# 256-token stages of a two-block transformer: high and low activations as one 512-column operand

## The chip, the cores and the metric

The kernel runs on one core of a Trainium2 chip. The metric is the device time of one execution in microseconds (us); less is better. The engines of a core work beside each other, each on an instruction queue of its own that it takes in order: TensorE (PE in the profile; PEld is its weight loads), VectorE (DVE), ScalarE (ACT), GpSimd (POOL), and SyncE (SP), whose queue issues the DMA loads of the weights.

## The reference

Everything is float32, with one batch of 256 latent tokens and width 1024. A first block of two layers works on the latent tokens and on 256 context tokens together; the context is dropped inside the second layer, after its mixer. A second block of one layer works on the 256 latent tokens alone. Cut to what the change touches:

```
swiglu(h, w_in, w_out):  a, b = split(h @ w_in);  return (silu(a) * b) @ w_out        # 1024 -> 2 x 2816 -> 1024

first_block, layer i = 0, 1:
    x_lat, x_ctx += 0.5 * gate * swiglu(modulate(x), ffn_a)
    o_l, o_c = mixer(h_l, h_c)        # neighbourhood attention + long convolution (0), retention (1)
    x_lat += gate * o_l
    x_lat += 0.5 * gate * swiglu(modulate(x_lat), ffn_b_in[i], ffn_b_out[i])
    # x_ctx likewise, but not after the mixer of layer 1

second_block:
    x = x + 0.5 * swiglu_2(rms_norm_2(x, g_ffn1), w_ffn1_gu, w_ffn1_down)
    q, k, v = split(rms_norm_2(x, g_mix) @ w_in)          # 16 heads: 12 dilated, 4 block attention
    x = x + concat(rms_norm_2(oa), rms_norm_2(ob)) @ w_out
    x = x + memory_cross_attention(x, mem, ...)           # q = h @ w_cq, k, v = mem_norm @ w_ckv, out @ w_co
    x = x + 0.5 * swiglu_2(rms_norm_2(x, g_ffn2), w_ffn2_gu, w_ffn2_down)
    return rms_norm_2(x, g_final)
```

## The kernel before

**Layout.** Activations lie with features on the partitions, in blocks of 128, and tokens along the row: `x[0]` to `x[7]` are the residual stream. The first block's joint stages have 512 token columns (latent and context); the stages behind the mixer of layer 1 have 256. These 256-token stages are: the second feed-forward of layer 1, both feed-forwards of block 2, the q and k projections of its mix, the memory keys (`mem_piece`), and the query and output projections of the cross attention.

**High and low parts.** Each float32 operand is kept as two parts in a reduced type: `split` has ScalarE copy the value into the high part (L152) and VectorE subtract that from the value into the low part (L153). A product of one block of K (128 features) with one block of 128 outputs is `mm3`, three matmuls into one PSUM accumulation: low weight by high activation (L200), high by low (L201), high by high (L202). For a 512-token stage the parts are tiles of their own; for 256 tokens, `pair` puts the high part into the left and the low part into the right half of one 512-column tile (tiles `h` for inputs, `g` for the products of the feed-forward).

**Weights.** SP loads them into `st` tiles (6 buffers); `split` makes `w` tiles of them (22 buffers), each [128, 512], so that one holds the high or the low parts for four products. A split can be made when TensorE has freed a `w` tile. PSUM has four tags, `pa` to `pd`, with two buffers of one bank, [128, 512], each.

**Feed-forward** (`ffn`). The 22 column blocks go in three groups (`GROUPS`: 8, 8 and 6 blocks), and within a group by pairs. For each block, eight products go into `pa` (gate) and eight into `pb` (up). The result is evacuated by VectorE and ScalarE into the tiles `t1` and `t2` (L645 without, L647 to L650 with a norm), and split into `g`. After each group `project_out` multiplies its `g` blocks with the rows of the second weight that belong to them, output block by output block into `pc`, and `residual` adds each bank to its `x` tile (L562). In the last group the sums of squares of the new `x` are gathered in `acc` (L350, L353, L354).

**Late norm.** In block 2 the reciprocal root mean square is not known yet when a stage starts. `norm_late` scales `x` by the gain and splits it (L517, L518); the sums over `acc` on TensorE (L205, into `pd`), the power on GpSimd (L365) and the spread over the partitions (copied at L537 into `rb[1]`) come while the first products already run: `settle` puts them behind certain accumulations, and the first four accumulations take K blocks 0 to 5 first, 6 and 7 later. The factor `rb[1]`, one for each token, is multiplied at the evacuation. The feed-forward of layer 1 has its norm applied beforehand (`rb` is None).

**Three lines elsewhere** that the rows show: L1352 is ScalarE's copy of a bank of memory keys; in the mix's attention, L1261 is GpSimd's addition of bias tables in SBUF and L1281 VectorE's scaling of the probabilities.

**Order.** The program is written in the order above; Tile's scheduler then puts the instructions of each engine in order, by their dependences and place in the program. So an engine's queue mixes stages, for instance weight splits for later products between the evacuations of this one.

## Time and profile before

| | before |
|---|---|
| time, median of 3 runs (lowest to highest) | 2554.69 us (2551.87 to 2554.76) |
| span of the profiled execution, from the first to the last instruction | 2549.0 us |
| the span's distance to the median | 5.7 us |
| TensorE busy | 2515.0 us (99%) |
| VectorE busy | 1751.8 us (69%) |
| ScalarE busy | 1109.4 us (44%) |
| GpSimd busy | 70.8 us (3%) |
| read from HBM | 382.8 MB, 153 GB/s over the span |
| chain of work that ended last | 82% of it TensorE |

Of the profiled execution the time between its first and its last instruction is known, and it is 2549.0 us; what lies around it is seen only as the distance to the runs' median. An engine counts as busy from the start of an instruction to its end; matmuls overlap, and their ends are modelled, so the distance from start to start says more on TensorE's pace than its busy time. A name such as L200 is a line of the kernel before; the rows of one line can have more than one shape.

### The profile page before, as it was taken

What the parts mean: (1) busy time and instruction counts of PE and PEld (TensorE: products, weight loads), DVE (VectorE), ACT (ScalarE), POOL (GpSimd) and SP (SyncE); (2) the same over time, 40 slices, a digit from 0 to 9 for tenths busy, and PEclk for the clock granted to TensorE, in tenths of its full rate; (3) what the DMA queues carried; (4) which work ended last, traced back from release to release, by engine and by line L of the source; (5) the groups of instructions that cost most, each with busy time, mean ns of one, the idle gap of its engine ahead of it and who ended that gap; (6) DMA issues with size and microseconds to landing.
All of it is one profiled execution on the core that took longest, in us unless ns stands there. A gap on an engine that the chain in (4) does not pass through costs nothing.

```text
span 2549.0 us, 39425 instructions
## 1 busy us (share of the span) xinstructions
PE 2515.0 (99%) x14967; PEld 2176.7 (85%) x14967; DVE 1751.8 (69%) x3443; ACT 1109.4 (44%) x2164; POOL 70.8 (3%) x95
## 2 busy tenths in 40 slices
PE   8998999999999999999999999999999999999999
PEld 5786778857987888988788888889999999789998
DVE  6896875577887747777533846667667667676775
ACT  4322224364432323432322635546556555665554
POOL 0000000210000000000000000000000000300000
PEclk9998999999999999999999999999999999999999
DMA  7575653331355635365422524435556556544553
GB/s 270 193 225 158 194 187 96 95 83 50 100 174 181 190 116 157 115 197 179 143 83 90 167 83 133 133 113 190 181 174 194 182 172 195 164 132 142 183 184 98
DMA packets 345133, 388.44 MB, mean 152 GB/s; under 512 B 22123, under 2 KB 294720, under 8 KB 344944
## 3 DMA queue, kind: packets, MB, share of 16 engines
q1 hardware_dynamic: 341752, 380.75, 47.6%
q10 hardware_dynamic: 3192, 5.18, 0.8%
q8 instruction: 117, 1.92, 0.3%
q14 instruction: 72, 0.59, 0.1%
HBM read 382.80 MB, written 6.23 MB: 153 GB/s over the span
## 4 chain that ended last, share of the span: by engine, by line
PE 82%; issue 8%; DVE 5%; DMA 4%; ACT 1%; POOL 0%; SPq 0%; POOLq 0%; DVEq 0%; ACTq 0%
PE pa L200 11%; PE pa L201 11%; PE pa L202 11%; PE pc L200 8%; PE pc L201 8%; PE pc L202 8%; PE pb L200 6%; PE pb L201 6%; PE pb L202 6%; DMA st<-in_w_mod_dram 2%; PE pb L205 2%; DVE t L308 2%; PE pc L205 2%; PE pd L205 1%; DVE w L153 1%
## 5 line engine op out<-in xcount | busy, mean ns | idle before, releaser
L152 ACT ACTIVATE w<-st 128x512 fp32r<-128x512 f32 (+1 forms) x1136 | 693.3, 620 | 872.3 <-PE pc L200 272.4
L153 DVE TENSOR_TENSOR w<-st,w 128x512 fp32r<-128x512 f32 (+1 forms) x1136 | 761.0, 677 | 340.0 <-ACT w L152 327.6
L200 PE MATMUL pa<-h,w 128*128 128x256 f32 (+1 forms) x1544 | 514.1, 333 | 0.2 <-ACT h L401 0.2
L202 PE MATMUL pa<-h,w 128*128 128x256 f32 (+1 forms) x1544 | 509.8, 330 | 0.0
L200 PE MATMUL pc<-g,w 128*128 128x256 f32 (+1 forms) x1404 | 444.0, 317 | 4.1 <-DVE w L153 1.7
L201 PE MATMUL pc<-g,w 128*128 128x256 f32 (+1 forms) x1404 | 443.1, 316 | 0.9 <-DVE g L153 0.9
L202 PE MATMUL pc<-g,w 128*128 128x256 f32 (+1 forms) x1404 | 441.8, 315 | 0.0
L201 PE MATMUL pa<-h,w 128*128 128x256 f32 (+1 forms) x1352 | 439.4, 325 | 0.0
L200 PE MATMUL pb<-h,w 128*128 128x256 f32 (+1 forms) x1120 | 371.0, 331 | 0.0
L202 PE MATMUL pb<-h,w 128*128 128x256 f32 (+1 forms) x1120 | 370.5, 331 | 0.0
L308 DVE SCALAR_TENSOR_TENSOR t<-st,cs,t 128x512 f32<-128x512 f32 x448 | 319.3, 745 | 40.9 <-DMA st<-in_w_mod_dram 39.3
L200 PEld LDWEIGHTS pa<-h,w 128*128 128x128 f32 x1544 | 294.0, 191 | 42.8 <-ACT w L152 8.7
L202 PEld LDWEIGHTS pa<-h,w 128*128 128x128 f32 x1544 | 294.1, 191 | 30.1 <-issue 4.6
L201 PE MATMUL pb<-h,w 128*128 128x256 f32 (+1 forms) x928 | 298.6, 322 | 0.0
L200 PEld LDWEIGHTS pc<-g,w 128*128 128x128 f32 x1404 | 267.2, 191 | 25.7 <-issue 5.4
L201 PEld LDWEIGHTS pc<-g,w 128*128 128x128 f32 x1404 | 267.8, 191 | 18.7 <-DVE g L153 2.4
L202 PEld LDWEIGHTS pc<-g,w 128*128 128x128 f32 x1404 | 267.7, 191 | 16.6
L201 PEld LDWEIGHTS pa<-h,w 128*128 128x128 f32 x1352 | 258.0, 191 | 24.7 <-issue 5.9
L200 PEld LDWEIGHTS pb<-h,w 128*128 128x128 f32 x1120 | 213.0, 190 | 20.1 <-DVE w L153 0.7
L202 PEld LDWEIGHTS pb<-h,w 128*128 128x128 f32 x1120 | 213.0, 190 | 19.8 <-issue 0.6
L201 PEld LDWEIGHTS pb<-h,w 128*128 128x128 f32 x928 | 176.9, 191 | 13.3 <-issue 0.2
L562 DVE SCALAR_TENSOR_TENSOR x<-pc,gate,x 128x256 f32<-128x256 f32 x212 | 95.5, 479 | 61.2 <-PE pc L202 60.7
(320 smaller groups left out, 2711.3 us busy)
## 6 DMA issues: line engine op xcount, KB each, us to landing
st<-in_w_mod_dram SPq DMA_DIRECT2D x128, 512.0 KB
st<-in_ffn_a_in_dram SPq DMA_DIRECT2D x88, 512.0 KB
st<-in_ffn_b_in_dram SPq DMA_DIRECT2D x88, 512.0 KB
st<-in_w_ffn_gu_dram SPq DMA_DIRECT2D x88, 512.0 KB
st<-in_ret_in_dram SPq DMA_DIRECT2D x48, 512.0 KB
st<-in_ffn_a_out_dram SPq DMA_DIRECT2D x40, 512.0 KB
st<-in_ffn_b_out_dram SPq DMA_DIRECT2D x40, 512.0 KB
st<-in_w_ffn_down_dram SPq DMA_DIRECT2D x40, 512.0 KB
```

What stands on the lines that cost most here:

```text
L152: self.nc.scalar.activation(hi, src, AF.Copy)
L153: self.nc.vector.tensor_sub(lo, src, hi.bitcast(FT))
L200: mm(out, ll, rh, start=start, stop=False, skip_group_check=True)
L201: mm(out, lh, rl, start=False, stop=False, skip_group_check=True)
L202: return mm(out, lh, rh, start=False, stop=stop, skip_group_check=True)
L205: return self.nc.tensor.matmul(out, lhsT, rhs, start=start, stop=stop, skip_group_check=True)
L308: nc.vector.scalar_tensor_tensor(acc[q, s], sts[k // 2][:, k % 2], c, acc[q, s], op0=OP.mult, op1=OP.add)
L562: nc.vector.scalar_tensor_tensor(xs, p, gate(c, s), xs, op0=OP.mult, op1=OP.add)
```

## The change

In the 256-token stages the tile with both parts is used as one operand. `pair` returns it along with its halves (`Halves.both`). The new `mmw` replaces the three matmuls of a product by two: the high weight by both halves, 512 columns, into the whole PSUM bank, and the low weight by the high half, 256 columns, into the bank's left half. So the left half holds high by high plus low by high, and the right half high by low. The halves are summed when the bank is read: by the new `join` (ScalarE copies the right half to SBUF, VectorE adds the left half), or, in `residual`, by adding the two halves to `x` one after the other. In `ffn` the evacuation of a 256-token stage is now: join of gate and up, with a late norm a multiplication by `rb[1]` on GpSimd for each, silu on ScalarE, product on VectorE. The q and k evacuations of the mix, the cross query and the memory keys go through `join` too. Where a stage has 512 tokens `mm3` stays.

```diff
@@ -84,6 +84,12 @@
         tile, o = self.at[ix[1], cols.start // self.blk]
         return tile[:, o:o + cols.stop - cols.start]
+
+
+class Halves(tuple):
+
+
+    both = None
...
@@ -156,7 +162,9 @@
             return alloc(FR), alloc(FR)
         a = alloc(FR)
-        return a[:, :256], a[:, 256:]
+        pair = Halves((a[:, :256], a[:, 256:]))
+        pair.both = a
+        return pair
...
@@ -201,6 +209,17 @@
         return mm(out, lh, rh, start=False, stop=stop, skip_group_check=True)
 
+    def mmw(self, out, lh, ll, pair, start, stop):
+
+        mm = self.nc.tensor.matmul
+        mm(out, lh, pair.both, start=start, stop=False, skip_group_check=True)
+        return mm(out[:, :256], ll, pair[0], start=False, stop=stop, skip_group_check=True)
+
+    def join(self, dst, p, part):
+
+        self.nc.scalar.activation(part, p[:, 256:], AF.Copy)
+        self.nc.vector.tensor_add(dst, p[:, :256], part)
+
...
@@ -559,17 +578,23 @@
             c = 2 * cg + i
             xs = self.x[c][:, 256 * s:256 * s + 256]
-            nc.vector.scalar_tensor_tensor(xs, p, gate(c, s), xs, op0=OP.mult, op1=OP.add)
+            for o in range(0, p.shape[-1], 256):
+                nc.vector.scalar_tensor_tensor(xs, p[:, o:o + 256], gate(c, s), xs, op0=OP.mult, op1=OP.add)
             if final:
                 self.sq_add(("x", s), xs, c == 0)
 
     def project_out(self, w, kts, rhs, ns, gate, final=True, after=None, tag="c"):
         kn = kts if kts <= 8 else kts // 2
+        wide = ns == 1 and getattr(rhs(0), "both", None) is not None
 
         def product(ws, cg, s0, n, pss, between=None):
             for c in range(2):
                 for k0, (wh, wl) in ws:
                     for k in range(kn):
+                        if wide:
+                            self.mmw(pss[c], wh[:, k, 128 * c:128 * c + 128], wl[:, k, 128 * c:128 * c + 128], rhs(k0 + k),
+                                     k0 + k == 0, k0 + k == kts - 1)
+                            continue
...
@@ -586,7 +611,7 @@
             product(ws, cg, 0, 256 * ns, pss)
             for s in range(ns):
-                self.residual(cg, s, [p[:, 256 * s:256 * s + 256] for p in pss], gate, final)
+                self.residual(cg, s, [p if wide else p[:, 256 * s:256 * s + 256] for p in pss], gate, final)
...
@@ -625,8 +650,8 @@
                             for p, (wh, wl) in zip(pss[j], (wg, wu)):
                                 for k in ks:
-                                    self.mm3(p[:, :256], wh[:, k, 128 * j:128 * j + 128], wl[:, k, 128 * j:128 * j + 128],
-                                             hs[k][0], hs[k][1], k == 0, k == KT - 1)
+                                    self.mmw(p, wh[:, k, 128 * j:128 * j + 128], wl[:, k, 128 * j:128 * j + 128],
+                                             hs[k], k == 0, k == KT - 1)
...
@@ -634,20 +659,25 @@
                         for p, (wh, wl) in zip(pss[j], (wg, wu)) if not done and (ns == 2 or c) else ():
                             for k in range(KT):
-                                self.mm3(p[:, sl], wh[:, k, 128 * j:128 * j + 128], wl[:, k, 128 * j:128 * j + 128],
-                                         hs[k][0][:, sl], hs[k][1][:, sl], k == 0, k == KT - 1)
+                                wk = wh[:, k, 128 * j:128 * j + 128], wl[:, k, 128 * j:128 * j + 128]
+                                if ns == 1:
+                                    self.mmw(p, *wk, hs[k], k == 0, k == KT - 1)
+                                else:
+                                    self.mm3(p[:, sl], *wk, hs[k][0][:, sl], hs[k][1][:, sl], k == 0, k == KT - 1)
                             if j == 0 and segs == [0] and ns == 2:
                                 self.settle()
                         s = self.t("1")
                         m = self.t("2")
-                        if rb is None:
+                        if ns == 1:
+                            for t, p in zip((s, m), pss[j]):
+                                self.join(t[:, sl], p, t[:, 256:])
+                                if rb is not None:
+                                    nc.gpsimd.tensor_tensor(t[:, sl], t[:, sl], rb[1], op=OP.mult)
+                            nc.scalar.activation(s[:, sl], s[:, sl], AF.Silu)
+                            nc.vector.tensor_mul(m[:, sl], m[:, sl], s[:, sl])
+                        else:
                             nc.scalar.activation(s[:, sl], pss[j][0][:, sl], AF.Silu)
                             nc.vector.tensor_mul(m[:, sl], s[:, sl], pss[j][1][:, sl])
-                        else:
-                            nc.vector.tensor_mul(s[:, sl], pss[j][0][:, sl], rb[1])
-                            nc.scalar.activation(s[:, sl], s[:, sl], AF.Silu)
-                            nc.vector.tensor_mul(m[:, sl], pss[j][1][:, sl], rb[1])
-                            nc.vector.tensor_mul(m[:, sl], m[:, sl], s[:, sl])
...
@@ -744,20 +774,24 @@
         for j in range(nt):
             p = self.ps("a")
+            wide = getattr(hs[0], "both", None) is not None
             for k in range(KT):
-                self.mm3(p[:, sl], wh[:, k, 128 * j:128 * j + 128], wl[:, k, 128 * j:128 * j + 128],
-                         hs[k][0][:, sl], hs[k][1][:, sl], k == 0, k == KT - 1)
-            evac(j, p[:, sl])
+                wk = wh[:, k, 128 * j:128 * j + 128], wl[:, k, 128 * j:128 * j + 128]
+                if wide:
+                    self.mmw(p, *wk, hs[k], k == 0, k == KT - 1)
+                else:
+                    self.mm3(p[:, sl], *wk, hs[k][0][:, sl], hs[k][1][:, sl], k == 0, k == KT - 1)
+            evac(j, p if wide else p[:, sl])
 
     def proj_pair(self, hs, w, items):
         ws = [self.wcols(w, 0, 8, c0, 256) for c0, _ in items]
-        ps = [[self.ps(t)[:, :256] for _ in range(2)] for t in "ab"]
+        ps = [[self.ps(t) for _ in range(2)] for t in "ab"]
         for ks in (range(6), range(6, KT)):
             for i, (wh, wl) in enumerate(ws):
                 for j in range(2):
                     for k in ks:
-                        self.mm3(ps[i][j], wh[:, k, 128 * j:128 * j + 128], wl[:, k, 128 * j:128 * j + 128],
-                                 *hs[k], k == 0, k == KT - 1)
+                        self.mmw(ps[i][j], wh[:, k, 128 * j:128 * j + 128], wl[:, k, 128 * j:128 * j + 128],
+                                 hs[k], k == 0, k == KT - 1)
...
@@ -1216,10 +1250,14 @@
         for i in range(4):
             def q_evac(j, p):
-                nc.vector.scalar_tensor_tensor(qT[i][:, j, :], p, 0.125, norm[1], op0=OP.mult, op1=OP.mult)
+                t = self.t("1")
+                self.join(t[:, :256], p, t[:, 256:])
+                nc.vector.scalar_tensor_tensor(qT[i][:, j, :], t[:, :256], 0.125, norm[1], op0=OP.mult, op1=OP.mult)
 
             def k_evac(j, p):
-                nc.vector.tensor_mul(kT[i][:, j, :], p, norm[1])
+                t = self.t("2")
+                self.join(t[:, :256], p, t[:, 256:])
+                nc.vector.tensor_mul(kT[i][:, j, :], t[:, :256], norm[1])
...
@@ -1349,7 +1387,7 @@
 
             def evac(j, p):
-                nc.scalar.activation(self.mk[i][:, j, :], p, AF.Copy)
+                self.join(self.mk[i][:, j, :], p, self.t("1")[:, :256])
...
@@ -1367,7 +1405,9 @@
         def q_evac(h):
             def f(j, p):
-                nc.vector.scalar_tensor_tensor(qs[h][:, j, :], p, 0.0625, norm[1], op0=OP.mult, op1=OP.mult)
+                t = self.t("1")
+                self.join(t[:, :256], p, t[:, 256:])
+                nc.vector.scalar_tensor_tensor(qs[h][:, j, :], t[:, :256], 0.0625, norm[1], op0=OP.mult, op1=OP.mult)
```

Line numbers shift with the edit: the lines of `split` are now L158 and L159, those of `mmw` L215 and L216, of `join` L220 and L221, the late-norm multiplication L675, silu L676, the product L677, the residual L582, the low half of `h` L537, and the addition to `acc` L373. Three places of the engines' orders follow. A number behind a name is that tile's in its program.

TensorE where the first output projection of block 2's first feed-forward comes to its last block of K: before, `pc_19036` and `pc_19037` are the banks of output blocks 0 and 1, `g_18903` is the product block that was evacuated last.

```order
L202 MATMUL pc_19036<-g_18902,w_19024 128x256
L200 MATMUL pc_19036<-g_18903,w_19025 128x256
L200 MATMUL pc_19037<-g_18417,w_19029 128x256
L201 MATMUL pc_19037<-g_18417,w_19028 128x256
L202 MATMUL pc_19037<-g_18417,w_19028 128x256
L201 MATMUL pc_19036<-g_18903,w_19024 128x256
L202 MATMUL pc_19036<-g_18903,w_19024 128x256
```

The same place on TensorE with the change; the banks are `pc_18488` and `pc_18489`, the last product block is `g_18379`.

```order
L216 MATMUL pc_18488<-g_18378,w_18477 128x256
L215 MATMUL pc_18489<-g_17965,w_18480 128x512
L216 MATMUL pc_18489<-g_17965,w_18481 128x256
L215 MATMUL pc_18489<-g_17966,w_18480 128x512
L216 MATMUL pc_18489<-g_17966,w_18481 128x256
L215 MATMUL pc_18489<-g_18110,w_18480 128x512
L216 MATMUL pc_18489<-g_18110,w_18481 128x256
L215 MATMUL pc_18489<-g_18111,w_18480 128x512
L216 MATMUL pc_18489<-g_18111,w_18481 128x256
L215 MATMUL pc_18489<-g_18244,w_18484 128x512
L215 MATMUL pc_18488<-g_18379,w_18476 128x512
L216 MATMUL pc_18488<-g_18379,w_18477 128x256
```

Before, one product of the next output block stood between the first and the second matmul on the last product block; now nine matmuls of the next output block stand ahead of the first of them.

ScalarE at that place, before: the silu of the last block (L648), splits of weights (`w`), and the high half of the last product block.

```order
L648 ACTIVATE t1_19008<-t1_19008 128x256
L152 ACTIVATE w_19168<-st_19162 128x512
L152 ACTIVATE w_19172<-st_19160 128x512
L152 ACTIVATE w_19176<-st_19162 128x512
L152 ACTIVATE g_18903<-t2_19009 128x256
```

The same with the change; L220 is the copy of a bank's right half, `pa_18376` for gate and `pb_18377` for up.

```order
L220 ACTIVATE t1_18456<-pa_18376 128x256
L158 ACTIVATE w_18592<-st_18586 128x512
L676 ACTIVATE t1_18456<-t1_18456 128x256
L158 ACTIVATE w_18596<-st_18584 128x512
L220 ACTIVATE t2_18457<-pb_18377 128x256
L158 ACTIVATE w_18600<-st_18586 128x512
L158 ACTIVATE g_18379<-t2_18457 128x256
```

A weight split stands ahead of each of the two copies and of the high half; before, ScalarE had nothing to do for the up product.

VectorE at the end of the same feed-forward, before: the residual additions to `x6` and `x7`, between them weight splits, the sum of squares and the low halves of the mix's input `h`.

```order
L562 SCALAR_TENSOR_TENSOR x6_100<-pc_20907,half_119,x6_100 128x256
L153 TENSOR_TENSOR w_21149<-st_21144,w_21148 128x512
L354 TENSOR_TENSOR acc_20755<-acc_20755,t3_20946 128x256
L518 SCALAR_TENSOR_TENSOR h_20959<-x6_100,colc_711,h_20959 128x256
L153 TENSOR_TENSOR w_21153<-st_21146,w_21152 128x512
L562 SCALAR_TENSOR_TENSOR x7_101<-pc_20908,half_119,x7_101 128x256
L153 TENSOR_TENSOR w_21157<-st_21144,w_21156 128x512
L354 TENSOR_TENSOR acc_20755<-acc_20755,t3_20950 128x256
```

The same place with the change.

```order
L582 SCALAR_TENSOR_TENSOR x6_100<-pc_20049,half_119,x6_100 128x256
L537 SCALAR_TENSOR_TENSOR h_20090<-x5_99,colc_711,h_20090 128x256
L582 SCALAR_TENSOR_TENSOR x6_100<-pc_20049,half_119,x6_100 128x256
L159 TENSOR_TENSOR w_20158<-st_20143,w_20157 128x512
L582 SCALAR_TENSOR_TENSOR x7_101<-pc_20050,half_119,x7_101 128x256
L373 TENSOR_TENSOR acc_19916<-acc_19916,t3_20077 128x256
L582 SCALAR_TENSOR_TENSOR x7_101<-pc_20050,half_119,x7_101 128x256
L537 SCALAR_TENSOR_TENSOR h_20091<-x6_100,colc_711,h_20091 128x256
L159 TENSOR_TENSOR w_20261<-st_20256,w_20260 128x512
L373 TENSOR_TENSOR acc_19916<-acc_19916,t3_20082 128x256
```

Each `x` has two additions, one for each half of its bank, and two weight splits instead of three stand between the first addition to `x6` and the last sum of squares, with two low halves of `h` instead of one.

## Rows read from the trace of the kernel before

**Rows 1.** The page: span, and each engine's busy us, share and instructions.

```profile
span 2549.0 us, 39425 instructions
...
PE 2515.0 (99%) x14967; PEld 2176.7 (85%) x14967; DVE 1751.8 (69%) x3443; ACT 1109.4 (44%) x2164; POOL 70.8 (3%) x95
```

**Rows 2.** Windows: length, then busy us (instructions) by engine, clock, DMA share, GB/s.

```profile
core 0: us, PE busy (x) PEld busy (x) DVE busy (x) ACT busy (x) POOL busy (x), PEclk, DMA share, GB/s
894.60:980.70 86.10, 86.10 (x382) 71.29 (x381) 46.04 (x80) 23.48 (x39) 0.00 (x0) 1.00 0.42 127
1984.60:2053.10 68.50, 68.50 (x573) 68.50 (x573) 48.24 (x88) 35.45 (x63) 0.00 (x0) 1.00 0.58 182
1937.00:2128.00 191.00, 191.00 (x1589) 190.54 (x1588) 139.05 (x266) 104.22 (x197) 0.70 (x1) 1.00 0.59 183
```

**Rows 3.** Timeline of TensorE, ends of the first two windows: start us, busy us.

```profile
894.23 0.40 PE L201 MATMUL pa<-f,w 128*128 128x512 f32 x1
...
980.63 0.39 PE L201 MATMUL pb<-f,w 128*128 128x512 f32 x1
...
1984.43 0.28 PE L200 MATMUL pc<-g,w 128*128 128x256 f32 x1
...
2053.05 0.28 PE L201 MATMUL pc<-g,w 128*128 128x256 f32 x1
```

**Rows 4.** Timeline of TensorE where 512 and 256 columns meet.

```profile
652.48 0.39 PE L202 MATMUL pa<-h,w 128*128 128x512 f32 x1
652.71 0.28 PE L200 MATMUL pc<-g,w 128*128 128x256 f32 x1
652.82 0.65 PE L200 MATMUL pa<-h,w 128*128 128x512 f32 x2
```

**Rows 5.** Waits from 1937 to 2128: us in total, times, longest us.

```profile
ACT w L152 <- PE pa L200: 27.2, 38, 2.0
```

**Rows 6.** Lines by form: busy us, mean ns, then idle time before and its releaser.

```profile
L1352 ACT ACTIVATE f<-pa 128x256 f32<-128x256 f32 x8 | 3.0, 372 | 2.8 <-PE pa L202 2.8
...
L152 ACT ACTIVATE g<-t 128x256 fp32r<-128x256 f32 x74 | 30.0, 408 | 5.5 <-DVE t L645 2.3 <-DVE t L650 1.8
...
L562 DVE SCALAR_TENSOR_TENSOR x<-pc,half,x 128x256 f32<-128x256 f32 x48 | 23.2, 483 | 17.3 <-PE pc L202 17.2
...
L649 DVE TENSOR_TENSOR t<-pb,g 128x256 f32<-128x256 f32 x44 | 18.7, 424 | 12.6 <-PE pb L202 12.5
```

**Rows 7.** Instructions of three lines in the mix: ns min/median/max, first and last start.

```profile
L1261 POOL TENSOR_TENSOR h<-h,g x16: 719/733/1241, 2197.2 to 2219.8; 128x256 f32<-128x256 f32 x16
...
L1281 DVE TENSOR_SCALAR t<-t,sa x32: 274/344/845, 2200.3 to 2244.4; 128x128 f32<-128x128 f32 x16, 128x256 f32<-128x256 f32 x16
...
L153 DVE TENSOR_TENSOR w<-st,w x3: 679/694/745, 2203.4 to 2210.4; 128x512 fp32r<-128x512 f32 x3
```

**Rows 8.** Timelines of ScalarE, VectorE and TensorE around 1981 to 1984.

```profile
1980.90 0.63 ACT L152 ACTIVATE w<-st 128x512 fp32r<-128x512 f32 x1 [0.81 <-PE pb L200]
1982.34 0.63 ACT L152 ACTIVATE w<-st 128x512 fp32r<-128x512 f32 x1 [0.81 <-PE pc L200]
...
1981.57 0.69 DVE L153 TENSOR_TENSOR w<-st,w 128x512 fp32r<-128x512 f32 x1
...
1983.62 0.42 DVE L153 TENSOR_TENSOR g<-t,g 128x256 fp32r<-128x256 f32 x1
...
1980.94 0.28 PE L200 MATMUL pc<-g,w 128*128 128x256 f32 x1
...
1984.09 0.38 PE L201 MATMUL pc<-g,w 128*128 128x256 f32 x1
```

**Rows 9.** Timelines of VectorE and TensorE at the feed-forward's end.

```profile
2126.44 0.48 DVE L562 SCALAR_TENSOR_TENSOR x<-pc,half,x 128x256 f32<-128x256 f32 x1
2126.84 0.68 DVE L153 TENSOR_TENSOR w<-st,w 128x512 fp32r<-128x512 f32 x1
2127.46 0.42 DVE L354 TENSOR_TENSOR acc<-acc,t 128x256 f32<-128x256 f32 x1
...
2129.93 0.50 PE L205 MATMUL pd<-cst,acc 128*128 128x1 f32 x4
```

## The prediction

> **What bounds the kernel now.** I read the page first. TensorE is busy for 2515.0 of 2549.0 us [rows 1], so time is only won where TensorE issues less or waits less. The second view is busy time by window: in the feed-forward of block 2 that fills 1937 to 2128 us, TensorE is busy for all of 191.00 us, VectorE for 139.05, ScalarE for 104.22, and the granted clock is 1.00, the higher of its two levels (2.4 GHz) [rows 2]. A TensorE that is always busy may still be slow for what it does, so the third view is the timeline, for the distance from one matmul's start to the next. Each end of two unbroken stretches is shown, with the counts in the windows. With 512 columns, 382 matmuls start between 894.23 and 980.63 us: 86.40 us over 381 steps, 226.8 ns. With 256 columns, 573 start between 1984.43 and 2053.05: 68.62 us over 572 steps, 120.0 ns [rows 2, 3]. Half the columns cost more than half the time. If the cost is linear in the columns, there is a fixed part of 2 x 120.0 - 226.8 = 13.2 ns in each matmul. The few places where the two sizes alternate show the same steps: 0.23 us after a 512, 0.11 after a 256 [rows 4]. So the price belongs to the matmul, not to its neighbours.
>
> Is anything else close to the limit? In that feed-forward ScalarE's weight splits wait mostly for TensorE to free a weight tile, 27.2 us behind pa alone [rows 5]. The weights are ready ahead, and neither DMA nor the splits set the pace.
>
> **The change part by part.** It replaces three 256-column matmuls for each product (one block of K, one block of 128 outputs) by one of 512 and one of 256. Products by the code: each of three feed-forwards has 22 column blocks x 2 (gate, up) x 8 blocks of K = 352, and 8 x 22 = 176 on the way out, so 528; 3 x 528 = 1584. Add 128 for q and k of the mix, 64 for cross q, 64 for cross out, 64 for the memory keys: 1904. One product takes 360.0 ns now and 226.8 + 120.0 = 346.8 then, so TensorE gets back 1904 x 13.2 ns = **25.1 us**. The columns streamed are the same 768, the saving is one fixed part per product. PSUM does not run out: a bank is allocated whole already.
>
> The Trainium skill speaks against this. "TensorE: Matmul & The Clock Gate", section "Back-to-back issue gap", gives a warm gap of N / 2.4 + 2.5 ns, so only 2.5 ns would be saved per product and 1904 x 2.5 = 4.8 us in all, an estimate from that page. The rows above have 13.2 and decide; what the page would make of the time is a rival below.
>
> Added: the two halves of a bank have to be summed. I cost that where TensorE could wait for it.
>
> (a) In the steady part of a feed-forward it costs nothing. Per output block of 16 products (5.55 us), ScalarE gets two copies of PSUM (0.37 each, as L1352) and VectorE the same number of additions as before of multiplications (0.42, as L649) [rows 6]; the multiplications by the norm go to GpSimd, two per block at 0.73 [rows 7]. The cover is the second buffer of pa and pb: a bank is wanted again three accumulations later, 3 x 8 x 0.347 = 8.3 us, against about 2 us until the addition has read it. In the projections with pa alone the room is one accumulation, 2.8 us; still enough.
>
> (b) At the start of each output projection the last product block is needed soon. Now: the projection starts at 1980.94; a weight split stands on ScalarE at 1980.90, VectorE's low half lands at 1983.62 + 0.42 = 1984.04; TensorE takes the last K block at 1984.09, where 25 matmuls at 0.12 would have brought it at 1983.94 [rows 8]: a wait of 0.15, at about six such places 0.9 us in all. With the change the order on ScalarE puts the copy of the up product behind that same split. Walking it from 1980.94: split until 0.50, copy until 0.87; VectorE subtracts for the weights at 0.63 to 1.24 (it did at 1981.57), adds until 1.66; GpSimd 1.70 to 2.42; VectorE subtracts for the split that stands at 1982.34, until 2.63, multiplies until 3.05; high half (0.41) and low half (0.42) with hops until about 3.95. TensorE's order now lets 14 + 9 matmuls go first, 4.04 us. So the first two groups of a feed-forward are a tie, for which I take 0.25 each between 0 and 1.5 (GpSimd's longest multiply is 1.24 [rows 7], and a subtraction may be caught behind it). The third group has 6 blocks of K, and only 10 + 8 matmuls, 3.12 us, go first: 0.8. Two feed-forwards with the norm at the end: 2 x (0.25 + 0.25 + 0.8) = 2.6, less 0.9: **+1.7 us**. The feed-forward of layer 1 has no multiplication on GpSimd, its chain is about 1 us shorter, and I take nothing (0 to 0.5 each).
>
> (c) Each residual addition becomes two, 0.48 each [rows 6]. In the last group VectorE has, from x0's first addition to the last sum of squares, by the order 16 residuals, 7 sums, 7 low halves of h and 9 weight subtractions. Spaced as at 2126.44, 2126.84, 2127.46 (0.40, 0.62, and 0.40 also for sums and h) that is 17.6 us, in which TensorE does 42 products and three matmuls of the next stage, 15.1: 2.5 behind. Now the same count gives 15.6 against 15.1, 0.5 behind, and the trace has the sum finished at 2127.88, that is 2.2 us after x7's products (36 matmuls before 2129.93) [rows 9]: 1.7 more than counted. So 4.2 us then, and TensorE asks for it after 21 matmuls, 3.6 us. A wait of 0.5 at each of two stage ends (into the first feed-forward of block 2 and into the mix), between 0 and 2: **+1.0 us**. The next things late there, the last two blocks of h, are wanted 7.8 us after, and are covered.
>
> (d) At the end of the kernel nothing hides the second half of x7's addition: **+0.4 us** (0.40 to 0.48 between its start and the next).
>
> Sum: -25.1 + 1.7 + 1.0 + 0.4 = -22.0 us. On the profiled span 2549.0 - 22.0 = 2527.0. The median of the runs, 2554.69, lies 5.7 above that span, so the time is 2554.7 - 22.0 = **2532.7 us**.
>
> **The rivals.**
>
> *Evacuation takes back half.* ScalarE's queue is in order. Where a copy falls behind one more weight split, it waits for the next tile TensorE frees, every four products, 1.39 us. At nine group starts: 12.5 us, so 2545.2. For it: ScalarE's idle time is mostly just that wait [rows 5]. Against: the walk in (b) has the split in front of the copy already, and it still fits.
>
> *The fixed part is not saved,* because an operand twice as wide carries both. Then the three costs stay alone: 2554.7 + 3.1 = 2557.8, which is within 0.2% of no change. Against it are the steps of the 512-column stages. By the page's gap the time would be 2554.7 - 4.8 + 3.1 = 2553.0, no measurable change either; the trace does not agree, its 256-column step is 120.0.
>
> *Slower: GpSimd holds VectorE.* The 88 multiplications run beside a VectorE that is busy for 139 of 191 us. In the mix, where GpSimd adds biases, VectorE's L1281 has a median of 344 ns and goes up to 845, and GpSimd's L1261 goes from 719 to 1241 [rows 7]. Per feed-forward VectorE then has 139.0 + 24 x 0.48 = 150.6, and TensorE offers 191.0 - 528 x 0.0132 = 184.0. If every multiplication stops VectorE for 0.73, it has 182.7 and nothing happens; for 1.24, it has 205.2, and TensorE waits 21.2 us in each of the two: 2554.7 - 25.1 + 42.4 + 1.4 = 2573.4. It decides from 1.03 us per multiplication on. Against it: the weight subtractions, VectorE's main work there, took 679 to 745 ns beside GpSimd's additions, hardly more than elsewhere [rows 7].
> The Trainium skill has the rule: "SBUF — State Buffer", "Who interferes with whom", says VectorE and GpSimd share a port pair as an exclusive lock, also for a two-input VectorE instruction against a GpSimd read. The L1281 row agrees that something of the kind exists; the three subtractions do not show it.
>
> *All of the gain, no waits:* -25.1 - 0.9 + 0.4 = -25.6, 2529.1.
>
> **How the numbers follow.** Forecast 0.70 (its own range 2529 to 2540), all of it 0.10, half taken back 0.13, nothing saved 0.03, GpSimd holds VectorE 0.04. A measurement here tells about 0.2%, 5.1 us, from no change; so faster 0.70 + 0.10 + 0.13 = 0.93, same 0.03, slower 0.04. Low end: 2529.1 less the 2 us that the runs before scatter below their median, 2527. High end: (b) at 1.5 for six starts and 0.5 for three, (c) at 4, (d) at 0.8 give -25.1 + 9.6 + 4 + 0.8 = -10.7, 2544; with little chance beyond 2543 except the rivals, 2543.
>
> **What would show it.** In the 256-token stages starts alternate 0.227 and 0.120; the windows keep TensorE at full. A wait at the last K block of an output projection should name VectorE's low half; at the sums of squares, VectorE; few of either above 1 us. Wrong would be: steps of 0.24 beside 0.12, ScalarE copies waiting more than 1.4 us, or VectorE's subtractions well over 0.7 us wherever L675 runs.

## The result, and the profile after

The change made the kernel slower: 2575.79 us (median of 4 runs, 2573.81 to 2578.42) against 2553.29 us for the kernel before (4 runs), ratio 1.0089, 95% interval 1.0075 to 1.0104. The forecast was 2532.7 with a range of 2527 to 2543, so it has the wrong sign. The profiled execution of the kernel after is the slowest of its four (2578.42 us, with a span of 2576.6) and that of the kernel before a short one (span 2549.0), so the spans lie 27.6 us apart and the medians 22.5.

The page of the kernel after, as in [rows 1]; below it the group of the wide matmuls that write `pc`, from the groups by line and form (busy us, mean ns, then the idle time before them and what ended it).

```profile
span 2576.6 us, 36146 instructions
...
PE 2515.9 (98%) x13063; PEld 2085.3 (81%) x13063; DVE 1808.3 (70%) x3599; ACT 1142.9 (44%) x2320; POOL 164.8 (6%) x183
...
L215 PE MATMUL pc<-g,w 128*128 128x512 f32 x592 | 226.0, 420 | 26.6 <-DVE g L159 25.2 <-DVE x L582 1.3
```

TensorE waits 25.2 us for VectorE's low half of a product block. In the kernel before its trace shows this wait in the 256-token stages only as four starts that come 0.27 us after the one ahead instead of 0.12, 0.6 us in all ([rows 8] has the first). Where the 25.2 us lie, and what comes with it, the windows show. The first is block 2's first feed-forward, the next two each eight column blocks (128 products) of unbroken products, the last three a start of an output projection with its wait and what follows.

```profile
core 0: us, PE busy (x) PEld busy (x) DVE busy (x) ACT busy (x) POOL busy (x), PEclk, DMA share, GB/s
1935.46:2143.85 208.39, 196.52 (x1064) 169.02 (x1063) 150.56 (x290) 111.53 (x241) 47.78 (x45) 0.95 0.54 168
...
1811.08:1856.31 45.23, 45.23 (x258) 39.24 (x257) 32.88 (x64) 29.71 (x62) 0.00 (x0) 1.00 0.61 190
...
2434.32:2478.70 44.38, 44.38 (x259) 39.13 (x258) 29.21 (x57) 25.29 (x57) 14.43 (x13) 1.00 0.57 176
...
1980.08:1986.27 6.19, 2.26 (x11) 1.71 (x11) 3.44 (x7) 2.90 (x7) 2.31 (x2) 0.95 0.52 167
1986.27:1992.40 6.13, 6.13 (x19) 5.26 (x20) 3.76 (x7) 1.87 (x4) 0.00 (x0) 0.50 0.34 108
1992.40:2007.63 15.23, 15.23 (x88) 13.21 (x87) 11.98 (x21) 6.36 (x11) 0.00 (x0) 1.00 0.56 166
```

Three things are to be seen. While products run, TensorE is faster than before, as meant: 128 products take 45.23 us (353.4 ns each) or 44.38 (346.7), against 360.0. At the start of the output projection it then stands for most of 6.19 us. And after that its granted clock is 0.50 (1.2 GHz) for 6.13 us, though TensorE has work all the time. Such a pair of wait and low clock stands at each of the six output projections of the two feed-forwards with the late norm; the stretches at 0.50 last 5.5 to 6.1 us, 35.7 in all. A product takes 0.640 us in them, from start to start, so about 45% of that time, 16.2 us, is lost. The six waits are 22.5 of the 25.2 us; the rest are three of 0.7 to 1.1 us, each some six us ahead of one of the six.

The sum over the spans: about 1130 products at 353.4 and 775 at 346.7 ns give back 17.8 us; the waits behind the low half cost 25.2 - 0.6, the low clock 16.2, waits for a bank of `pc` 1.3. That is +24.3 of the 27.6 us between the spans (2576.6 - 2549.0); most of the rest is that the starts around each of these waits lie some 0.27 us further apart than the idle time in its record says.

**Why the low half is late.** One column block's evacuation ahead of that start, by the timelines of ScalarE, VectorE, GpSimd and TensorE:

```profile
1979.12 0.42 ACT L158 ACTIVATE g<-t 128x256 fp32r<-128x256 f32 x1 [1.43 <-DVE t L677]
1979.44 0.37 ACT L220 ACTIVATE t<-pa 128x256 f32<-128x256 f32 x1
...
1981.68 0.42 ACT L676 ACTIVATE t<-t 128x256 f32<-128x256 f32 x1 [1.35 <-POOL t L675]
1982.00 0.61 ACT L158 ACTIVATE w<-st 128x512 fp32r<-128x512 f32 x1
1982.52 0.36 ACT L220 ACTIVATE t<-pb 128x256 f32<-128x256 f32 x1
...
1985.34 0.42 ACT L158 ACTIVATE g<-t 128x256 fp32r<-128x256 f32 x1 [1.94 <-DVE t L677]
...
1979.60 0.42 DVE L159 TENSOR_TENSOR g<-t,g 128x256 fp32r<-128x256 f32 x1
1979.94 0.42 DVE L221 TENSOR_TENSOR t<-pa,t 128x256 f32<-128x256 f32 x1
1980.36 0.69 DVE L159 TENSOR_TENSOR w<-st,w 128x512 fp32r<-128x512 f32 x1
...
1983.26 0.42 DVE L221 TENSOR_TENSOR t<-pb,t 128x256 f32<-128x256 f32 x1
1983.59 0.68 DVE L159 TENSOR_TENSOR w<-st,w 128x512 fp32r<-128x512 f32 x1
1984.88 0.43 DVE L677 TENSOR_TENSOR t<-t,t 128x256 f32<-128x256 f32 x1 [0.61 <-POOL t L675]
1985.79 0.42 DVE L159 TENSOR_TENSOR g<-t,g 128x256 fp32r<-128x256 f32 x1 [0.48 <-ACT g L158]
...
1980.43 1.21 POOL L675 TENSOR_TENSOR t<-t,g 128x256 f32<-128x256 f32 x1 [1.81 <-DVE t L221]
1983.75 1.10 POOL L675 TENSOR_TENSOR t<-t,g 128x256 f32<-128x256 f32 x1 [2.11 <-DVE t L221]
...
1981.94 0.40 PE L215 MATMUL pc<-g,w 128*128 128x512 f32 x1
1986.27 0.80 PE L215 MATMUL pc<-g,w 128*128 128x512 f32 x1 [3.94 <-DVE g L159]
```

Follow ScalarE. Its queue holds, in this order, the copy of the gate bank, the silu, the copy of the up bank, the high half. The silu waits for GpSimd's first multiplication (1.21 us); the copy of the up bank stands behind the silu, although its products are long done; GpSimd's second multiplication (1.10) can only start behind that copy and its addition; the high half waits for it; and the next block's gate copy stands behind the high half. So a block goes once round this loop, from one gate copy to the next, with both multiplications in series. The two low halves shown, which end these rounds, start 6.19 us apart; in the steady part of the next group it is 6.25, where TensorE makes a block's 16 products in 5.65. Each block is 0.6 us later than the one before, and at the end of eight the output projection needs the last one at once.

GpSimd's multiplication was expected at 0.73. In the loop it takes 1.1 to 1.2, with a weight subtraction of VectorE beside it. Where GpSimd starts first, the same two instructions share the time the other way round (timelines of VectorE and GpSimd, early in the next group):

```profile
2018.32 1.26 DVE L159 TENSOR_TENSOR w<-st,w 128x512 fp32r<-128x512 f32 x1
...
2018.30 0.73 POOL L675 TENSOR_TENSOR t<-t,g 128x256 f32<-128x256 f32 x1 [2.40 <-DVE t L221]
```

Whoever comes first has its usual time, and the other is held. In the loop VectorE comes first: its subtraction stands right behind the addition on which GpSimd waits. By the timelines that is so for 73 of the 88 multiplications, which take 0.83 to 1.29 us. In 13 GpSimd is first; 11 of these take 0.74, and the subtraction beside them 0.98 to 1.27. Whether the long multiplications come from the subtractions, e8 below tests.

### The profile page after: what moved, and what is told of

Same layout as the page of the kernel before. It is cut to its first block, busy times and chain, and to the rows that moved or that the text cites. A ratio compares the mean times of both kernels' runs of the same rounds, so it can differ in the third digit from the quotient of the medians.

```text
span 2576.6 us, 36146 instructions
## 1 busy us (share of the span) xinstructions
PE 2515.9 (98%) x13063; PEld 2085.3 (81%) x13063; DVE 1808.3 (70%) x3599; ACT 1142.9 (44%) x2320; POOL 164.8 (6%) x183
## 4 chain that ended last, share of the span: by engine, by line
PE 90%; DVE 4%; DMA 3%; ACT 1%; issue 1%; POOL 1%; SPq 0%; POOLq 0%; DVEq 0%; ACTq 0%
PE pa L208 9%; PE pa L210 9%; PE pa L209 9%; PE pa L215 7%; PE pc L208 6%; PE pc L209 6%; PE pc L210 6%; PE pc L215 6%; PE pb L215 5%; PE pb L210 4%; PE pb L208 4%; PE pb L209 4%; PE pa L216 3%; PE pc L216 3%; PE pb L216 3%; PE pb L224 2%
## 5 line engine op out<-in xcount | busy, mean ns | idle before, releaser
L158 ACT ACTIVATE w<-st 128x512 fp32r<-128x512 f32 (+1 forms) x1136 | 689.7, 619 | 784.1 <-PE pc L208 190.0
L159 DVE TENSOR_TENSOR w<-st,w 128x512 fp32r<-128x512 f32 (+1 forms) x1136 | 768.0, 684 | 325.2 <-ACT w L158 305.5
L208 PE MATMUL pa<-h,w 128*128 128x512 f32 (+1 forms) x792 | 300.0, 380 | 0.1
L210 PE MATMUL pa<-h,w 128*128 128x512 f32 (+1 forms) x792 | 296.9, 375 | 0.0
L208 PE MATMUL pc<-g,w 128*128 128x512 f32 (+1 forms) x812 | 276.4, 341 | 3.2 <-DVE w L159 1.7
L209 PE MATMUL pc<-g,w 128*128 128x512 f32 (+1 forms) x812 | 274.8, 339 | 0.1
L210 PE MATMUL pc<-g,w 128*128 128x512 f32 (+1 forms) x812 | 274.2, 338 | 0.0
L215 PE MATMUL pa<-h,w 128*128 128x512 f32 x752 | 268.7, 396 | 0.0
L215 PE MATMUL pc<-g,w 128*128 128x512 f32 x592 | 226.0, 420 | 26.6 <-DVE g L159 25.2
L209 PE MATMUL pa<-h,w 128*128 128x512 f32 (+1 forms) x600 | 225.7, 377 | 0.0
L210 PE MATMUL pb<-h,w 128*128 128x512 f32 (+1 forms) x560 | 211.8, 378 | 0.0
L208 PE MATMUL pb<-h,w 128*128 128x512 f32 (+1 forms) x560 | 211.6, 378 | 0.0
L216 PE MATMUL pa<-h,w 128*128 128x256 f32 x752 | 211.5, 282 | 0.0
L215 PE MATMUL pb<-h,w 128*128 128x512 f32 x560 | 200.6, 397 | 0.0
L208 PEld LDWEIGHTS pa<-h,w 128*128 128x128 f32 x792 | 149.8, 189 | 41.1 <-ACT w L158 8.4
L210 PEld LDWEIGHTS pa<-h,w 128*128 128x128 f32 x792 | 149.6, 189 | 30.4 <-issue 4.6
L208 PEld LDWEIGHTS pc<-g,w 128*128 128x128 f32 x812 | 153.9, 190 | 24.9 <-issue 5.4
L216 PE MATMUL pc<-g,w 128*128 128x256 f32 x592 | 172.4, 293 | 0.0
L209 PEld LDWEIGHTS pc<-g,w 128*128 128x128 f32 x812 | 154.0, 190 | 17.1 <-DVE g L159 0.9
L215 PEld LDWEIGHTS pa<-h,w 128*128 128x128 f32 x752 | 141.2, 188 | 32.7 <-ACT w L158 0.3
L210 PEld LDWEIGHTS pc<-g,w 128*128 128x128 f32 x812 | 153.9, 190 | 16.6
```

What stands on the lines that cost most here:

```text
L158: self.nc.scalar.activation(hi, src, AF.Copy)
L159: self.nc.vector.tensor_sub(lo, src, hi.bitcast(FT))
L208: mm(out, ll, rh, start=start, stop=False, skip_group_check=True)
L209: mm(out, lh, rl, start=False, stop=False, skip_group_check=True)
L210: return mm(out, lh, rh, start=False, stop=stop, skip_group_check=True)
L215: mm(out, lh, pair.both, start=start, stop=False, skip_group_check=True)
```

## The experiments

Theory A, which the expectations below go by: the loop through ScalarE's queue, with the slow multiplications in it, is longer than TensorE's block. The rivals: B, GpSimd stops VectorE, which becomes the bound (the slower rival of the prediction); C, reading a bank in two halves costs it, whichever engine multiplies; D, the wide matmuls themselves cost it. The kernel before stood at 2552.3 to 2553.0 us (medians) beside these runs. The table has, for the second group of block 2's first feed-forward, by the timelines: the time between two blocks' ends on TensorE, between two blocks' low halves, and the longest wait of TensorE behind a product block's high or low half at the group's output projection.

| kernel | us (median) | ratio to before, 95% interval | TensorE's block | low half to low half | wait |
|---|---|---|---|---|---|
| before | 2553.29 | | 5.76 | 5.76 | 0.15 |
| after | 2575.79 | 1.0089 (1.0075 to 1.0104) | 5.65 | 6.25 | 3.97 |
| e2: added evacuations alone | 2595.89 | 1.0173 (1.0159 to 1.0187) | 5.76 | 6.53 | 5.27 |
| e3: up multiplied on VectorE | 2560.60 | 1.0028 (1.0016 to 1.0040) | 5.55 | 5.99 | 3.56 |
| e4: up copied by VectorE | 2546.10 | 0.9978 (0.9969 to 0.9987) | 5.65 | 5.46 and 5.85 in turn | 0.68 |
| e8: no low weights | 2544.66 | 0.9969 (0.9957 to 0.9981) | 5.65 | 5.65 | 0.22 |
| e1: both multiplied on VectorE | 2541.26 | 0.9959 (0.9947 to 0.9972) | 5.65 | 5.65 | none |

The wait is there where the low halves come further apart than TensorE's blocks, and grows with that distance; where they keep step it is 0.7 us or less in this group. At the other five places e4 and e8 still have single waits of up to 1.4 and 1.7 us.

**e1, the multiplication on VectorE.**

```
-                                    nc.gpsimd.tensor_tensor(t[:, sl], t[:, sl], rb[1], op=OP.mult)
+                                    nc.vector.tensor_mul(t[:, sl], t[:, sl], rb[1])
```

> The changed kernel with the late-norm multiplication on VectorE instead of GpSimd; all else as changed. Theory A (the evacuation of a block is one loop through ScalarE's queue, with two GpSimd multiplications of 1.1 to 1.2 us in it: 6.2 us a block against 5.6 of TensorE's products; the lag comes out as 4 to 5 us of waiting at each of six output projections, and TensorE's clock is low for some us after): the loop is 1.5 us shorter, no lag builds up, waits at the six places under 1 us each, 2532 to 2541 us. Theory C (reading two halves costs it, through copies that stand behind weight splits, whichever engine multiplies): the waits stay, about 2570. Theory D (the wide matmuls themselves cost it): about 2570.

Measured 2541.26: C and D fall, since halves and wide matmuls are all still there. At seven output projections (those six and one of layer 1) another wait has come in the place of the first, here in the timelines of TensorE and VectorE:

```profile
1982.70 0.47 PE L215 MATMUL pc<-g,w 128*128 128x512 f32 x1 [0.93 <-DVE x L582]
...
1981.08 0.48 DVE L582 SCALAR_TENSOR_TENSOR x<-pc,half,x 128x256 f32<-128x256 f32 x1
1981.47 0.68 DVE L159 TENSOR_TENSOR w<-st,w 128x512 fp32r<-128x512 f32 x1
1982.07 0.87 DVE L582 SCALAR_TENSOR_TENSOR x<-pc,half,x 128x256 f32<-128x256 f32 x2
```

The third output block wants the first one's bank, and the second addition that frees it stands behind a weight subtraction: 0.9 to 1.4 us each, 7.1 in all, with the clock at 1.00 after it.

**e2, the added evacuations without the wide matmuls.**

```
-        mm(out, lh, pair.both, start=start, stop=False, skip_group_check=True)
-        return mm(out[:, :256], ll, pair[0], start=False, stop=stop, skip_group_check=True)
+        mm(out[:, :256], ll, pair[0], start=start, stop=False, skip_group_check=True)
+        mm(out[:, 256:], lh, pair[1], start=start, stop=False, skip_group_check=True)
+        return mm(out[:, :256], lh, pair[0], start=False, stop=stop, skip_group_check=True)
```

> The changed evacuations alone: each product is three matmuls of 256 columns again (low by high and high by high into the left half, high by low into the right), summed at the read as in the changed kernel. Theory A: TensorE's block is 5.76 us and the loop stays at 6.2, so 0.45 us of lag a block, some 3 us of waiting and as much of low clock at each of six places: 2575 to 2595 us. Theory C: the same. Theory D: as the kernel before, 2550 to 2558.

Measured 2595.89, by 0.9 us above A's range: the evacuations without the wide matmuls make the kernel 43 us slower than before. The loop was not 6.2 but 6.53 us, so the lag was larger too; D is out. The longer loop has a place in the timeline of ScalarE, where the edit brought a weight split between the high half and the next gate copy, which in the kernel after follow on each other (1979.12 and 1979.44 above):

```profile
2040.86 0.42 ACT L158 ACTIVATE g<-t 128x256 fp32r<-128x256 f32 x1 [1.58 <-DVE t L678]
2041.18 0.62 ACT L158 ACTIVATE w<-st 128x512 fp32r<-128x512 f32 x1
2041.70 0.36 ACT L221 ACTIVATE t<-pa 128x256 f32<-128x256 f32 x1
```

So this run changes the order of a queue as well as the matmuls, and its 43 us aren't the price of the evacuations in the order of the kernel after.

**e3, half of the multiplications on GpSimd.**

```
-                                    nc.gpsimd.tensor_tensor(t[:, sl], t[:, sl], rb[1], op=OP.mult)
+                                    eng = nc.gpsimd if t is s else nc.vector
+                                    eng.tensor_tensor(t[:, sl], t[:, sl], rb[1], op=OP.mult)
```

> As changed, but GpSimd multiplies the gate product alone, VectorE the up product. Theory A: a threshold; the loop is 0.75 us shorter, 5.5 against 5.6, so hardly any lag: waits of at most 1.5 us at the six places, 2534 to 2546 us. Theory B (GpSimd stops VectorE, which becomes the bound): half of the multiplications are left and about half of the loss, 2552 to 2558. Theory C: about 2570.

Measured 2560.60, outside A's range and nearer to B's. But the wait is still there behind a loop of 5.99 us against 5.55, so A's mechanism holds and its price was wrong: the loop got 0.26 us shorter, not 0.75. The timeline of VectorE shows why:

```profile
2041.48 0.42 DVE L676 TENSOR_TENSOR t<-t,g 128x256 f32<-128x256 f32 x1
2041.82 0.68 DVE L159 TENSOR_TENSOR w<-st,w 128x512 fp32r<-128x512 f32 x1
2042.42 0.42 DVE L678 TENSOR_TENSOR t<-t,t 128x256 f32<-128x256 f32 x1
```

Between the multiplication by the norm and that by the silu VectorE's queue has a weight subtraction. Beside a multiplication on GpSimd it cost the loop nothing of its own; now it lies in it.

**e4, the up bank's copy on VectorE.**

```
-                                self.join(t[:, sl], p, t[:, 256:])
+                                if rb is None or t is s:
+                                    self.join(t[:, sl], p, t[:, 256:])
+                                else:
+                                    nc.vector.tensor_copy(t[:, 256:], p[:, 256:])
+                                    nc.vector.tensor_add(t[:, sl], p[:, :256], t[:, 256:])
```

> As changed, GpSimd multiplying both, but in the feed-forwards with the late norm VectorE copies the right half of the up bank, not ScalarE; so that copy no longer stands behind the silu, which waits for GpSimd. VectorE gets 22 x 0.42 = 9 us more work in each of the two. Theory A: the two multiplications of a block follow on each other, the loop is about 4.5 us, no lag; 2534 to 2548 us. Theory B: VectorE has more to do and is still stopped, 2580 or more. Theory C: half of the copies are off ScalarE, about 2565.

Measured 2546.10, within A's range. GpSimd still multiplies both, and VectorE has more to do (in the first feed-forward 159.87 us in 192.40, against 150.56 in 208.39), yet the kernel is 30 us faster. B falls: VectorE was not the bound. That the copy stood behind the silu on ScalarE is what this edit takes away, as A expected.

**e8, no low weights.** The first weights of the two feed-forwards with the late norm are only copied; the high part is multiplied in place of the low one. Cut:

```
-                        tiles = self.w(), self.w()
+                        tiles = (self.w(),) * 2 if self.one_part else (self.w(), self.w())
...
+                    if self.one_part:
+                        self.nc.scalar.activation(parts[0], st[:, i:i + per, b * blk:b * blk + blk], AF.Copy)
```

> As changed, GpSimd multiplying; but the first weights of the two feed-forwards with the late norm get no low part: VectorE does not subtract for them, and the high part is multiplied in its place. Theory A with a shared resource (a multiplication takes 1.1 to 1.2 us because a subtraction of VectorE's stands on it): most multiplications take 0.73, the loop falls to about 5 us, waits at the six output projections under 1.5 us: 2532 to 2548 us. If 1.1 to 1.2 is GpSimd's own price here: durations stay, the loop is shorter only by what the subtractions took in VectorE's queue, and some wait is left: 2550 to 2565.

GpSimd's multiplications, first in the kernel after, then in this one (ns min/median/max, first and last start):

```profile
L675 POOL TENSOR_TENSOR t<-t,g x88: 732/1117/1293, 1942.9 to 2547.3; 128x256 f32<-128x256 f32 x88
```

```profile
L681 POOL TENSOR_TENSOR t<-t,g x88: 730/738/1287, 1941.1 to 2516.0; 128x256 f32<-128x256 f32 x88
```

Without the subtractions the median is 738 instead of 1117 ns, the low halves keep step with TensorE, and the time is 2544.66. The waits at the six output projections are 0.2 to 0.3 us, but for two of 1.7 in the second feed-forward. In this run 72 of the 88 have no weight subtraction beside them, and these take 0.73 to 0.75 us. So the 1.1 us are the price of the company, not of the instruction. Since the subtractions are also gone from VectorE's queue, this run doesn't say how much of the shorter loop is owed to each.

**e5, TensorE's pace alone.** The evacuations are those of the kernel before, on the left half of each bank, for instance:

```
-            for o in range(0, p.shape[-1], 256):
+            for o in (0,):
...
+                            nc.vector.tensor_mul(s[:, sl], pss[j][0][:, sl], rb[1])
```

> The wide matmuls alone: TensorE works as in the changed kernel, but every bank is read as in the kernel before, its left half only, so the high by low products are computed and left out of the sums. With no evacuation in the way TensorE's saving shows by itself. In the traces so far a product took either 346.7 or about 353 ns in a stretch, against 360.0 before. All at the first: 1904 x 13.3 = 25 us, 2527 us. All at the second: 1904 x 7 = 13 us, 2539 us. If the second pace comes from the added evacuations, it should be gone here: 2525 to 2530.

Measured 2533.50 (0.9930, 0.9916 to 0.9943; before 2552.28): 18.8 us saved. Both paces appear in this trace too, in the same stages as after, so they don't come from the added evacuations.

**e6, two wide matmuls, then two narrow ones**, on top of e1.

```
-        return mm(out[:, :256], ll, pair[0], start=False, stop=stop, skip_group_check=True)
+        self.held.append((out, ll, pair[0], stop))
+        if len(self.held) == 2:
+            for o, l, r, e in self.held:
+                mm(o[:, :256], l, r, start=False, stop=e, skip_group_check=True)
+            self.held = []
```

> The kernel with the multiplication on VectorE (e1_vector_norm), and the matmuls in another order: two wide ones, then their two narrow ones. That kernel ran about half of its products at 353 ns and half at 346.7. If the slower pace belongs to the change from 512 to 256 columns with every matmul, half as many changes leave 350 or 346.7 everywhere: about 6 us less, 2533 to 2538 us. If it has another cause: as that kernel, 2539 to 2544.

Measured 2537.44 (0.9944, 0.9931 to 0.9956), with e9 the fastest kernel that leaves nothing out. Windows of six blocks (96 products) in each of its three feed-forwards:

```profile
1822.40:1855.84 33.44, 33.44 (x195) 29.18 (x193) 24.64 (x48) 22.82 (x49) 0.00 (x0) 1.00 0.62 196
2009.95:2043.39 33.44, 33.44 (x194) 29.18 (x193) 28.69 (x61) 22.14 (x49) 0.00 (x0) 1.00 0.62 193
2416.92:2450.36 33.44, 33.44 (x194) 29.18 (x193) 28.68 (x61) 22.16 (x49) 0.00 (x0) 1.00 0.62 196
```

348.3 ns a product everywhere: with half as many changes of width the slower pace is gone. Why it is, the run doesn't show.

**e7, the output projections as before**, on top of e1.

```
-        wide = ns == 1 and getattr(rhs(0), "both", None) is not None
+        wide = False
```

> The kernel with the multiplication on VectorE, with the output projections as in the kernel before (three matmuls into the left half, one residual addition). In that kernel TensorE waited 0.9 to 1.4 us behind a residual addition at seven starts of an output projection, 7.2 us in all. If the second residual addition is what makes it wait, these go, and 592 products lose 7 to 13 ns each, 4 to 8 us: 2537 to 2545 us, and no wait behind the residual over 0.3 us. If the waits come from VectorE's other work, they stay: 2545 to 2550.

Measured 2543.51 (0.9965, 0.9951 to 0.9979). All seven waits behind the residual are gone. The timeline of e1 names the second addition for them; this run alone doesn't show it, since three matmuls a product also leave VectorE more time. The time is no better than e1's: what the output projections' wide products gave back is lost. How much that is can't be read from the two times, since nearly all of this run's wide products went at the slower pace, and about half of e1's.

**e9, the residual's right half copied by ScalarE**, on top of e6.

```
-            for o in range(0, p.shape[-1], 256):
-                nc.vector.scalar_tensor_tensor(xs, p[:, o:o + 256], gate(c, s), xs, op0=OP.mult, op1=OP.add)
+            parts = [p]
+            if p.shape[-1] == 512:
+                parts = [p[:, :256], self.t("4")[:, :256]]
+                nc.scalar.activation(parts[1], p[:, 256:], AF.Copy)
+            for part in parts:
+                nc.vector.scalar_tensor_tensor(xs, part, gate(c, s), xs, op0=OP.mult, op1=OP.add)
```

> The fastest version so far (e6_two_wide_two_narrow) with the residual read otherwise: ScalarE copies a bank's right half to SBUF, VectorE adds the left half from PSUM and then the copy, so the bank is free after one addition of VectorE, which no weight subtraction splits from a second. In e6 TensorE waited 0.6 to 1.2 us for a bank behind the second residual addition at seven places, 5.9 us in all. If the bank's release is what held it, these waits go: 2530 to 2534 us. If VectorE's backlog at the start of an output projection is what holds it, the one addition comes as late as before and the waits stay above 0.5 us: 2536 to 2539; slower than that if the copies stand behind weight splits on ScalarE.

Measured 2537.65 (0.9940, 0.9926 to 0.9953), as e6. The seven waits fell to 0.3 to 0.5 us, 3.1 in all against 5.9, and most of the 2.8 us was given back where a ScalarE instruction is now late at the kernel's end (timeline of TensorE):

```profile
2524.82 0.33 PE L1478 MATMUL pb<-cst,t 128*128 128x128 f32 x1 [0.93 <-ACT t L1474]
```

From the last product of an output projection to the end it takes 12.1 us, against 10.4 in e6.

## Why the prediction was wrong

**The step that failed is (a)**, that the added evacuation costs nothing in the steady part of a feed-forward. It set the time until a bank is read (about 2 us) against the time until the bank is wanted again (8.3 us). The 8.3 us were enough: TensorE never waited for pa or pb there. The 2 us held for the first block of a group only: by the timelines the up bank of the second group's first block was read 1.8 us after its products, that of the eighth 5.9 us after, for the lag had grown. The cover that counts is how often a block can be evacuated, not how soon a bank is free. The added work was summed by engine, and each engine had room; the waits between them, in queues that go in order, make a round of 6.25 us against 5.65, the 0.73 of a multiplication having become 1.12 in the median. The step needed one walk from a gate copy to the next gate copy.

**Step (b)** had the right place and the right witness (a wait for VectorE's low half), and a size of 2.6 us where 25.2 came out. The 0.9 that it took off for the kernel before is 0.6 in that trace, at four places. It began the walk at the output projection's start with the gate already through; in the trace the gate copy comes 2.4 us after that start, behind the previous block's high half. It took GpSimd at 0.72, though [rows 7] had 1.24 for such an instruction beside VectorE; the longer value was kept for the range only, as if rare, while here VectorE's subtraction came first in 73 of 88 cases. The low clock behind the long waits (16.2 us in all) was nowhere in the sum.

**The saving** was mis-sized: 25.1 forecast, 18.8 measured (e5; by the interval of its ratio 14.5 to 21.4). The rows that the 13.2 ns came from had no stretch with the widths in alternation but [rows 4], three matmuls long. In the slower of the two paces the steps of the kernel after are 0.233 to 0.241 us for a wide matmul and 0.113 to 0.120 for a narrow one, near the 0.24 beside 0.12 that the prediction named as a sign of being wrong; in the faster they are 0.230 and 0.117, as forecast.

**Step (c)** expected 0.5 us at two stage ends, and there no wait over 0.3 is found; the second addition showed instead as waits for a bank of `pc`, 1.3 us here and 7.1 in e1, which were not counted. **Step (d)**, 0.4 forecast: from the start of the last matmul of an output projection to the end it takes 10.41 us against 10.28, 0.13 more. **The distance of 5.7 us** from the profiled span to the median is mostly scatter between runs: where a run's time and its span are both known, they lie 1.8 us apart (2578.42 and 2576.6 here).

**The rivals.** "GpSimd holds VectorE" gave 2573.4 and was given 0.04. Its time is nearly the measured one, its mechanism isn't what happened: VectorE is busy for 150.56 of 208.39 us, as much as the prediction worked out without any holding (150.6), and not the bound, and e4 gives it more work and wins 30 us. The holding mostly goes the other way, and it takes ScalarE's queue to make it decide. The prediction also had two things wrong here. Its threshold, 1.03 us per multiplication, doesn't follow from its numbers: (184.0 - 150.6) / 44 is 0.76, just above the 0.73 that it reckoned with. And the three subtractions of [rows 7] were no sign against holding: they came first, and it was GpSimd's next addition that grew. These are the timelines of VectorE and GpSimd in the kernel before; L1260 is the smaller addition of bias tables, 0.46 us in the median.

```profile
2203.39 0.69 DVE L153 TENSOR_TENSOR w<-st,w 128x512 fp32r<-128x512 f32 x1
...
2204.89 0.74 DVE L153 TENSOR_TENSOR w<-st,w 128x512 fp32r<-128x512 f32 x1
...
2210.44 0.68 DVE L153 TENSOR_TENSOR w<-st,w 128x512 fp32r<-128x512 f32 x1
...
2203.50 0.90 POOL L1260 TENSOR_TENSOR h<-h,g 128x128 f32<-128x128 f32 x1
...
2205.05 0.90 POOL L1260 TENSOR_TENSOR h<-h,g 128x128 f32<-128x128 f32 x1
...
2210.47 1.24 POOL L1261 TENSOR_TENSOR h<-h,g 128x256 f32<-128x256 f32 x1
```

So the rows that the prediction held against this rival already showed the longer GpSimd instruction that the loop was to have. The Trainium skill's rule ("SBUF — State Buffer", "Who interferes with whom") of a lock between the two engines' shared port fits these rows, the pair at 2018 and the median of e8. "Evacuation takes back half" had the queue right, but let ScalarE wait for a tile from TensorE, not for GpSimd.

## What to carry to other kernels

When evacuation moves to more engines, don't only add up each engine's work: walk one block round, in the order of the queues, and compare that round with the time in which the producer makes a block. Here a lag of a tenth per block was invisible in TensorE's steady part and came due all at once where the last block was needed. An instruction moved to GpSimd to unload VectorE should be priced beside VectorE's traffic, not alone. And a wait of several microseconds on TensorE can cost more than its length: behind each of the six here stood a stretch at the lower clock.

## What the runs showed of the hardware

Three things had not been expected. TensorE's granted clock was 0.50 for 5.5 to 6.1 us after each of the six waits of 2.9 to 4.0 us in the kernel after, while behind waits of 0.9 to 1.7 us (e1, e8) it stayed at 1.00. The length of the wait alone does not decide it: in e3 the clock stayed at 1.00 behind a wait of 2.62 us and was 0.50 for 3.4 us behind one of 2.41, and in e4 for 3.2 us behind waits of 1.34 and 0.49 close together. A GpSimd multiplication of 128x256 and a VectorE subtraction of 128x512 take 0.73 and 0.69 us apart; beside each other the later one takes longer, 1.10 and 1.21 or 1.26 in the rows above. And a product of one wide and one narrow matmul has two paces, 353.4 and 346.7 ns, each of which lasts over whole stretches and changes only where stages or waits break them, with the clock at 1.00 in both. In pairs, two wide and two narrow, it is 348.3 everywhere. What sets the pace in a stretch stays open.
